# Linear ReLU attention: Q of the first octet loaded in fp32 on SP's queue

## The chip, the cores and the metric

The kernel runs on one core of a Trainium2 chip. The core has a matrix engine (TensorE, PE in the profile, with its weight loads as PEld), a vector engine (VectorE, DVE), a scalar engine (ScalarE, ACT), a general engine (GpSimd, POOL), a synchronising engine (SyncE, SP) and 16 DMA engines that move data between HBM and the on-chip memory SBUF. SP, ACT and POOL each issue DMA transfers on a queue of their own: q1 is SP's, q10 is ACT's and q0 is POOL's. PSUM is the memory that PE writes its results to.

The metric is the device time of one execution in microseconds; lower is better.

## The reference

```python
Q_feat = np.maximum(0, Q)
K_feat = np.maximum(0, K)
KV = np.einsum('bhkd,bhkv->bhdv', K_feat, V)
K_sum = np.sum(K_feat, axis=2)
numerator = np.einsum('bhqd,bhdv->bhqv', Q_feat, KV)
denominator = np.einsum('bhqd,bhd->bhq', Q_feat, K_sum)
return (numerator / (denominator[:, :, :, None] + 1e-10)).astype(np.float32)
```

Q, K and V are fp32 arrays of 8 batches x 12 heads x 512 rows x 64 values. That is 96 heads, 12.58 MB for each input and for the output.

## The kernel before

**Tiles.** Eight heads make an octet, and there are NO = 12 octets. An octet has two groups of four heads. K and V are loaded by group (g = 0 to 23): 128 partitions x 1024 values, which is 0.52 MB in HBM, in rows of 4 KB. Q is loaded by octet: 128 partitions x 2048 values, which is 1.05 MB in HBM, in rows of 8 KB. The output is stored by octet in the same form as Q.

**Loads.** POOL's DMAs (`load_kv`, lines 94 and 96, and `load_q`, line 100) cast fp32 to bf16 on the way, so they write half of the bytes that they read. K and V of the first two groups (F32 = 2) are the exception: SP loads K (line 106) and ACT loads V (line 107), both in fp32, into tiles `kv_first` that are borrowed from the pool `outp`, which later holds the output tiles `o_sb`. POOL's queue then runs in program order: Q of octet 0 (`load_q(0)`, line 108), the making of a bf16 identity matrix for transposes (`make_identity`, line 109), and for each octet from 1 to 11 two groups of K and V and then Q. The transfers of POOL's queue have eight semaphores in turn, so the ninth transfer is issued only when the first has landed, and so on. All of the instruction order is written out by hand (`manual_schedule`): each engine executes its instructions in the order of the program.

**Work on a group.** `prep(g)` (DVE, lines 136 and 138) takes relu of K with a mask per head into `kf` and copies one half of V into `vo`; `prep_v` (ACT, line 143, or DVE, line 145) copies the other half. `mm_kv(g)` (PE, line 150) multiplies 16 pairs of these into PSUM `ps_kv`, and `evac_kv` (ACT, line 160) copies the result into the bf16 tiles `kvd`. These are zeroed once, by DVE (`zero_kv`, line 129); in the order of DVE that stands after the work on groups 0 and 1 and after the fp32 identity `ident32` (line 259) and `mask_h` (line 261).

**Work on an octet.** `transp` (PE, line 171) transposes Q, two halves of 8 transposes each, into PSUM tiles `ps_qt` of the pool `pqt`. `relu_q` (ACT, line 179) takes relu of them into `qt`. `denom` (PE, line 210, then DVE, lines 213 to 222) computes the denominators and their reciprocals. `out_t` (PE, line 201, ACT, line 203) computes the transposed products in PSUM tiles of the pool `pou` (tag `ps_out`, two buffers) and copies them to SBUF. `back` (PE, line 228) transposes these in fp32 with `ident32` into tiles of the same tag, and `norm` (DVE, line 234) multiplies by the reciprocals into `o_sb`.

**Stores.** SP stores `o_sb` (line 249; the last octet in two halves, line 247). For octets 0 to 6 the store is preceded on SP's queue by a tiny transfer (line 242) that waits until K of the octet five further on (DELAY = 5) has landed. So the loads go ahead of the stores, and the stores of five octets are still to come when the loads are done.

**Order at the start.** PE runs `mm_kv(0)`, `mm_kv(1)`, then the transposes of Q of octet 0 and the steps above, octet by octet.

Of the kernel before, what the change touches and what calls it, by code (L numbers as in the profile page):

```python
# [10 lines left out]
def kernel(  # L11
# [7 lines left out]
    nc = tc.nc  # L19
    B, H, S, D = Q.shape  # L20
    assert D == 64
    P = 128
# [7 lines left out]
    U = RQ // 2  # L30
# [6 lines left out]
    fp32 = mybir.dt.float32  # L37
    bf16 = mybir.dt.bfloat16
# [3 lines left out]
    def pool(name, bufs, **kw):  # L42
        return ctx.enter_context(tc.tile_pool(name=name, bufs=bufs, **kw))
# [7 lines left out]
    outp = pool("outp", DELAY + 2)  # L51
    otp = pool("otp", 2)
    pkv = pool("pkv", 1, space=bass.MemoryType.PSUM)
    pqt = pool("pqt", 2, space=bass.MemoryType.PSUM)
    pde = pool("pde", 1, space=bass.MemoryType.PSUM)
    pou = pool("pou", 2, space=bass.MemoryType.PSUM)

    def view(X, f):
        return X.rearrange("b h s d -> (b h s d)").rearrange("(n p f) -> n p f", p=P, f=f)

    Qr, Kr, Vr, Or = view(Q, RQ * D), view(K, R * D), view(V, R * D), view(out, RQ * D)

    ident = consts.tile([P, P], bf16, name="ident")
    ident32 = consts.tile([P, P], fp32, name="ident32")
# [25 lines left out]
    q_sb, k_sb, v_sb = {}, {}, {}  # L90
# [7 lines left out]
    def load_q(o):  # L98
        q_sb[o] = qin.tile([P, U, 2 * D], bf16, name="q_sb")
        nc.gpsimd.dma_start(out=q_sb[o].rearrange("p u f -> p (u f)"), in_=Qr[o])  # L100


    for g in range(F32):
        kv = outp.tile([P, 2, R, D], fp32, name="kv_first", tag="o_sb")
        k_sb[g], v_sb[g] = kv[:, 0], kv[:, 1]
        nc.sync.dma_start(out=k_sb[g].rearrange("p r d -> p (r d)"), in_=Kr[g])
        nc.scalar.dma_start(out=v_sb[g].rearrange("p r d -> p (r d)"), in_=Vr[g])
    load_q(0)
    make_identity(nc, ident)
    for o in range(1, NO):  # L110
        load_kv(2 * o)
# [54 lines left out]


    def transp(o, i):
        ps = pqt.tile([P, U // 2, P], bf16, name="ps_qt")
        for u in range(U // 2):  # L170
            nc.tensor.transpose(ps[:, u, :], q_sb[o][:, i * (U // 2) + u, :], ident)  # L171
        return ps

    def relu_q(o, i, ps, eng=None):
# [6 lines left out]
    def qt(o):  # L181
        for i in range(2):
            relu_q(o, i, transp(o, i))
# [41 lines left out]
    def back(o, j):  # L225
        ps = pou.tile([P, 16, D], fp32, name="ps_bk", tag="ps_out")
        for v in range(8):
            nc.tensor.transpose(ps[:, 2 * v:2 * v + 2].rearrange("p c d -> p (c d)"),  # L228
                                ot[o][:, 8 * j + v].rearrange("p h c -> p (h c)"), ident32)
        return ps  # L230
# [20 lines left out]
    def out_tile():  # L251
        return outp.tile([P, RQ, D], fp32, name="o_sb", tag="o_sb")
# [50 lines left out]
    o = NO - 2  # L303
    g = 2 * NO - 2
# [9 lines left out]
    o_sb = out_tile()  # L314
    norm(o, 0, back(o, 0), o_sb)
    ps = back(o, 1)
    mm_kv(g + 1)
    evac_kv(o + 1, slice(1, 2), share=True)
    for i in range(2):
        relu_q(o + 1, i, transp(o + 1, i), nc.vector if i == 1 else None)  # L320
# [36 lines left out]
```

## Time and profile before

The runs took 126.66, 126.75 and 127.84 us; the median is 126.75 us. The profiled execution has a span of 124.8 us from its first instruction to its last; what a run takes beyond the span lies outside of it.

| what | in the profile before |
|---|---|
| median of the runs | 126.75 us |
| span of the profiled execution | 124.8 us |
| PE busy | 86.6 us (69%) |
| DVE busy | 81.1 us (65%) |
| ACT busy | 79.4 us (64%) |
| POOL busy | 31.2 us (25%) |
| DMA, bytes written | 32.68 MB, mean 262 GB/s |
| HBM read and written | 37.75 MB and 12.58 MB |
| POOL's queue q0 | 17.83 MB written |
| SP's queue q1 | 13.63 MB |
| ACT's queue q10 | 1.05 MB |

Busy time is the time in which an engine executes something; it is an average over stages that may have different limits. The DMA row of the page cuts the span into 40 slices and gives the mean busy share of the 16 DMA engines in tenths. GB/s counts written bytes; a casting load reads twice what it writes. A line of the timeline has the start in us, the duration, the engine, the line of the program, the operation, the tiles and, in brackets, how long the engine stood idle before and what ended that.

### The profile page before, as it was taken

The page shows a single profiled execution, that of the slowest core. Times are in us where ns is not written, and L with a number is a line of the kernel's source. Part 1 is how long each engine was busy: PE and PEld are TensorE (multiplying, and loading weights), DVE is VectorE, ACT ScalarE, POOL GpSimd, SP SyncE. Part 2 cuts the span into 40 slices and gives each one's busy share as a digit, 9 for nine tenths or more (in the row PEclk, how much of TensorE's full clock was granted, in tenths as well). Part 3 has the DMA queues.
Part 4 walks back from the last instruction along what each step waited for, and adds up shares of the span by engine and source line. Part 5 has one row for each costly group of instructions (what it writes and reads, how often), then busy time and mean ns, then how long its engine had stood idle before and what let it go on. Part 6 is the DMA issues. An engine that isn't in the chain of part 4 may idle for free.

```text
span 124.8 us, 2656 instructions
## 1 busy us (share of the span) xinstructions
PE 86.6 (69%) x1067; PEld 78.5 (63%) x1067; DVE 81.1 (65%) x176; ACT 79.4 (64%) x114; POOL 31.2 (25%) x62
## 2 busy tenths in 40 slices
PE   0032287998889899893598599399777577797600
PEld 0031285997878787792597499299576476695500
DVE  2257644759797997989147845934928918979430
ACT  0163369989898999988149558665939737737100
POOL 6902434314243331142133115034122000000000
PEclk9999999999999999999779859959999999999995
DMA  3999999999999999999999999999999999999993
GB/s 112 377 306 215 215 205 210 217 205 218 203 215 211 206 223 324 253 216 300 281 215 280 304 213 249 331 215 230 334 234 218 323 257 215 312 421 420 428 416 143
DMA packets 10748, 32.68 MB, mean 262 GB/s; under 512 B 1392, under 2 KB 1392, under 8 KB 9328
## 3 DMA queue, kind: packets, MB, share of 16 engines
q0 software_dynamic: 8064, 17.83, 74.7%
q1 hardware_dynamic: 2384, 13.63, 27.1%
q10 hardware_dynamic: 288, 1.05, 2.2%
q8 instruction: 8, 0.13, 0.4%
q14 instruction: 4, 0.03, 0.1%
HBM read 37.75 MB, written 12.58 MB: 403 GB/s over the span
## 4 chain that ended last, share of the span: by engine, by line
DMA 34%; DVE 30%; PE 23%; ACT 5%; issue 2%; DVEq 1%; SPq 0%; POOLq 0%; ACTq 0%
DMA v_sb<-in_V_dram 14%; DVE o_sb L234 13%; DMA q_sb<-in_Q_dram 13%; PE ps_kv L150 11%; DMA kv_first<-in_K_dram 7%; PE ps_bk L228 7%; DVE kf L136 5%; PE ps_qt L171 4%; DVE vo L138 3%; ACT kvd L160 2%; DVE vo L145 2%; PE ps_ot L201 2%; DVE den L218 2%; ACT qt L179 2%; DVE rec L222 1%
## 5 line engine op out<-in xcount | busy, mean ns | idle before, releaser
L150 PE MATMUL ps_kv<-vo,kf 128*128 128x132 bf16 x384 | 30.8, 244 | 17.7 <-ACT vo L143 8.2
L150 PEld LDWEIGHTS <-kf 128*128 128x128 bf16 x384 | 28.4, 110 | 19.0 <-DVE vo L138 10.9
L234 DVE TENSOR_TENSOR o_sb<-ps_bk,rec 128x1024 f32<-128x1024 f32 x24 | 28.3, 1219 | 17.1 <-PE ps_bk L228 17.1
L160 ACT CAST kvd<-ps_kv 64x260 bf16<-64x260 f32 (+1 forms) x54 | 18.7, 346 | 19.5 <-PE ps_kv L150 16.6
L203 ACT COPY ot_sb<-ps_ot 128x1024 f32<-128x1024 f32 x24 | 24.0, 1014 | 3.0 <-PE ps_ot L201 2.0
L179 ACT ACTIVATE qt<-ps_qt 128x1024 bf16<-128x1024 bf16 x23 | 22.4, 1026 | 5.6 <-PE ps_qt L171 5.5
L228 PE MATMUL ps_bk<-ident,ot_sb 128*128 128x128 f32 x192 | 23.0, 273 | 0.4 <-ACT ot_sb L203 0.4
L136 DVE TENSOR_SCALAR kf<-k_sb,mask 128x1024 bf16<-128x1024 bf16 x44 | 18.4, 460 | 6.4 <-DMA k_sb<-in_K_dram 6.3
L94 POOL DMA_DIRECT2D k_sb<-in_K_dram x22 | 11.9, 542 | 37.7 <-DMA q_sb<-in_Q_dram 24.1
L228 PEld LDWEIGHTS ps_bk<-ident,ot_sb 128*128 128x128 f32 x192 | 20.8, 141 | 0.7 <-ACT ot_sb L203 0.7
L171 PE MATMUL ps_qt<-ident,q_sb 128*128 128x128 bf16 x192 | 16.0, 250 | 6.0 <-DMA q_sb<-in_Q_dram 5.9
L171 PEld LDWEIGHTS <-q_sb 128*128 128x128 bf16 x192 | 14.3, 114 | 7.3 <-DMA q_sb<-in_Q_dram 7.1
L201 PE MATMUL ps_ot<-qt,kvd 128*128 128x256 bf16 x96 | 14.7, 283 | 5.0 <-DVE o_sb L234 4.3
L96 POOL DMA_DIRECT2D v_sb<-in_V_dram x22 | 12.3, 558 | 17.4 <-DMA k_sb<-in_K_dram 11.1
L201 PEld LDWEIGHTS <-kvd 128*128 128x128 bf16 x96 | 9.2, 101 | 7.8 <-issue 5.7
L138 DVE TENSOR_SCALAR vo<-v_sb,mask 128x1024 bf16<-128x1024 bf16 x22 | 10.6, 482 | 1.8 <-DMA v_sb<-in_V_dram 1.8
L143 ACT ACTIVATE vo<-v_sb,mask 128x1024 bf16<-128x1024 bf16 x10 | 11.5, 1152 | 0.2
L210 PEld LDWEIGHTS <-qt 128*128 128x128 bf16 x192 | 6.8, 97 | 4.4 <-ACT qt L179 3.4
L210 PE MATMUL ps_den<-kvd,qt 128*128 128x16 bf16 x192 | 7.5, 180 | 2.4 <-ACT qt L179 2.1
L100 POOL DMA_DIRECT2D q_sb<-in_Q_dram x12 | 6.6, 546 | 8.5 <-DMA v_sb<-in_V_dram 6.2
L213 DVE SCALAR_TENSOR_TENSOR own<-ps_den,mask_h 128x256 f32<-128x256 f32 x12 | 5.0, 417 | 3.3 <-PE ps_den L210 3.3
L136 DVE TENSOR_SCALAR kf<-kv_first,mask 128x1024 bf16<-128x1024 f32 x4 | 2.8, 749 | 5.1 <-DMA kv_first<-in_K_dram 5.1
(24 smaller groups left out, 28.3 us busy)
## 6 DMA issues: line engine op xcount, KB each, us to landing
out_dram<-o_sb SPq DMA_DIRECT2D x11, 1024.0 KB, 9.0
q_sb<-in_Q_dram POOLq DMA_DIRECT2D x12, 512.0 KB, 14.8
k_sb<-in_K_dram POOLq DMA_DIRECT2D x22, 256.0 KB, 14.1
v_sb<-in_V_dram POOLq DMA_DIRECT2D x22, 256.0 KB, 13.2
kv_first<-in_V_dram ACTq DMA_DIRECT2D x2, 512.0 KB, 7.2
kv_first<-in_K_dram SPq DMA_DIRECT2D x2, 512.0 KB, 6.9
out_dram<-o_sb SPq DMA_DIRECT2D x2, 512.0 KB, 4.3
scratch<-k_sb SPq DMA_DIRECT2D x7, 0.1 KB, 5.0
```

What stands on the lines that cost most here:

```text
L96: nc.gpsimd.dma_start(out=v_sb[g].rearrange("p r d -> p (r d)"), in_=Vr[g])
L136: nc.vector.tensor_scalar(kf[g][:, :, s, :], k_sb[g], scalar1=0.0, scalar2=mask[:, 0, s:s + 1], op0=Alu.max, op1=Alu.mult)
L138: nc.vector.tensor_scalar(vo[g % NB][:, :, 0, 2:D + 2], v_sb[g], scalar1=mask[:, 1, 0:1], scalar2=None, op0=Alu.mult)
L150: nc.tensor.matmul(ps_kv[:, g % 2, 0:2 * (D + 2)].rearrange("p (t d) -> p t d", t=2), kf[g][:, r, :, :].rearrange("p s d -> p (s d)"), vo[ ...
L160: copy(kvd[o % NK][64 * c:64 * c + 64, 4 * gs.start + s:4 * gs.stop:2, c * D1:c * D1 + D1].rearrange("p (g t) d -> p g t d", t=2), ps_kv[6 ...
L171: nc.tensor.transpose(ps[:, u, :], q_sb[o][:, i * (U // 2) + u, :], ident)
L179: nc.scalar.activation(to, ps, Act.Relu)
L201: nc.tensor.matmul(ps[:, i], kvd[o % NK][:, h, 1:2 * D + 1], q[:, :, h, :], start=True, stop=True, skip_group_check=True)
L203: nc.scalar.copy(ot[o][:, :, 4 * j:4 * j + 4], ps.rearrange("p h u c -> p u h c"))
L210: nc.tensor.matmul(ps[:, u], qt_sb[o % NZ][:, u, :], kvd[o % NK][:, :, 0:2 * D1:2 * D1 - 1], start=True, stop=True, skip_group_check=True)
L228: nc.tensor.transpose(ps[:, 2 * v:2 * v + 2].rearrange("p c d -> p (c d)"), ot[o][:, 8 * j + v].rearrange("p h c -> p (h c)"), ident32)
L234: nc.vector.tensor_tensor(o_sb[:, rs], ps, rec[o][:, rs].unsqueeze(2).to_broadcast([P, 16, D]), op=Alu.mult)
```

## The change

Q of octet 0 is no longer loaded by POOL with a cast. A tile `q_first` of the pool `outp` (same tag and size as `o_sb`) takes it in fp32, and SP loads it as its first transfer. K of group 0 moves from SP's queue to the head of ACT's, ahead of V of groups 0 and 1; K of group 1 stays on SP's queue, behind Q. On POOL's queue the making of the identity comes first, and then the loads from octet 1 on. The 16 transposes of octet 0 read fp32, use `ident32` in place of the bf16 identity, and write two fp32 tiles with the tag `ps_out` of the pool `pou`, which the products of `out_t` and `back` use as well. All other octets are as before. The lines after the change are numbered up to six higher than before.

```diff
--- before.py
+++ after.py
@@ -100,12 +100,15 @@
         nc.gpsimd.dma_start(out=q_sb[o].rearrange("p u f -> p (u f)"), in_=Qr[o])
 
 
+    q_first = outp.tile([P, U, 2 * D], fp32, name="q_first", tag="o_sb")
+    q_sb[0] = q_first
+    nc.sync.dma_start(out=q_first.rearrange("p u f -> p (u f)"), in_=Qr[0])
     for g in range(F32):
         kv = outp.tile([P, 2, R, D], fp32, name="kv_first", tag="o_sb")
         k_sb[g], v_sb[g] = kv[:, 0], kv[:, 1]
-        nc.sync.dma_start(out=k_sb[g].rearrange("p r d -> p (r d)"), in_=Kr[g])
+        eng = nc.scalar if g == 0 else nc.sync
+        eng.dma_start(out=k_sb[g].rearrange("p r d -> p (r d)"), in_=Kr[g])
         nc.scalar.dma_start(out=v_sb[g].rearrange("p r d -> p (r d)"), in_=Vr[g])
-    load_q(0)
     make_identity(nc, ident)
     for o in range(1, NO):
         load_kv(2 * o)
@@ -166,9 +169,12 @@
 
 
     def transp(o, i):
-        ps = pqt.tile([P, U // 2, P], bf16, name="ps_qt")
+        if o == 0:
+            ps = pou.tile([P, U // 2, P], fp32, name="ps_q0", tag="ps_out")
+        else:
+            ps = pqt.tile([P, U // 2, P], bf16, name="ps_qt")
         for u in range(U // 2):
-            nc.tensor.transpose(ps[:, u, :], q_sb[o][:, i * (U // 2) + u, :], ident)
+            nc.tensor.transpose(ps[:, u, :], q_sb[o][:, i * (U // 2) + u, :], ident32 if o == 0 else ident)
         return ps
 
     def relu_q(o, i, ps, eng=None):
```

## The prediction

> **What bounds the kernel now.** I read the page's DMA rows first, because the busiest engine, PE, fills only 69% of the span.
>
> ```profile
> DMA  3999999999999999999999999999999999999993
> HBM read 37.75 MB, written 12.58 MB: 403 GB/s over the span
> ```
>
> All 16 DMA engines work in every slice but the first and last. The traffic over HBM, 50.33 MB, is fixed by the inputs and the output. Next, the table by stretches (share of the DMA engines and GB/s stand last):
>
> ```profile
> 1.00:2.00 1.00, 0.00 (x0) 0.00 (x0) 0.44 (x9) 0.00 (x0) 0.76 (x2) 1.00 0.21 41
> 2.00:3.00 1.00, 0.00 (x0) 0.00 (x0) 0.17 (x2) 0.00 (x0) 0.93 (x4) 1.00 0.78 258
> 3.00:5.00 2.00, 0.00 (x0) 0.00 (x0) 0.00 (x0) 0.00 (x0) 2.00 (x4) 1.00 1.03 412
> ...
> 10.00:45.00 35.00, 27.15 (x349) 24.83 (x348) 26.11 (x59) 28.02 (x42) 12.60 (x23) 1.00 1.11 211
> 110.00:122.00 12.00, 6.90 (x86) 5.79 (x84) 7.10 (x11) 3.59 (x5) 0.00 (x0) 1.00 1.01 421
> ```
>
> GB/s counts bytes written. A casting load on POOL's queue writes half of what it reads, so 211 is 422 read. Fp32 loads give 412 and stores 421: whichever queue carries a byte, the rate is about 420. 50.33 MB at 420 GB/s are 119.8 us of the 124.8 us span; the rest is the ramp up to 3 us and the drain. The kernel is bound by DMA.
>
> Third, the DMA view of 5.3 to 9.5 us, where three queues compete (packets in all 324):
>
> ```profile
> q0 software_dynamic: 111, 0.45, 54.8%
> q10 hardware_dynamic: 114, 0.47, 27.5%
> q1 hardware_dynamic: 99, 0.37, 23.3%
> ```
>
> q0 is POOL's (here Q of octet 0, 8 KB read per row), q10 ACT's, q1 SP's (4 KB rows). The queues take turns by packet, so an 8 KB row gets twice the bytes of a 4 KB row. The same view of 1 to 5.3 us has no q0 at all: POOL issues Q at 1.24, and its data moves no sooner than 4.1 us later, while SP's and ACT's, issued at 0.74, start within about a microsecond.
>
> Fourth, the timeline of the start (start us, duration, engine, line; in brackets the idle time before and who ended it):
>
> ```profile
> 5.50 1.41 DVE L136 TENSOR_SCALAR kf<-kv_first,mask 128x1024 bf16<-128x1024 f32 x2 [3.12 <-DMA kv_first<-in_K_dram]
> 5.73 1.28 ACT L143 ACT_TABLE_LOAD   x1 [5.73 <-DMA kv_first<-in_V_dram]
> ...
> 10.25 1.42 DVE L136 TENSOR_SCALAR kf<-kv_first,mask 128x1024 bf16<-128x1024 f32 x2 [1.95 <-DMA kv_first<-in_K_dram]
> ...
> 13.61 1.09 ACT L160 CAST kvd<-ps_kv 64x130 bf16<-64x130 f32 x4 [1.71 <-DVE kvd L129]
> ...
> 14.76 1.92 PE L150 MATMUL ps_kv<-vo,kf 128*128 128x132 bf16 x16 [4.61 <-ACT kvd L160]
> ...
> 17.83 1.94 ACT L179 ACTIVATE qt<-ps_qt 128x1024 bf16<-128x1024 bf16 x2
> ```
>
> K of group 0 is there at 5.5, V at 5.7, K of group 1 at 10.25. Q of octet 0 is needed only at 16.5, long after it landed. Fifth, the Q transposes on PE in the timeline:
>
> ```profile
> 29.18 1.06 PE L171 MATMUL ps_qt<-ident,q_sb 128*128 128x128 bf16 x16
> ...
> 60.77 1.86 PE L171 MATMUL ps_qt<-ident,q_sb 128*128 128x128 bf16 x16 [2.89 <-DMA q_sb<-in_Q_dram]
> ...
> 80.77 1.42 PE L171 MATMUL ps_qt<-ident,q_sb 128*128 128x128 bf16 x16 [1.53 <-DMA q_sb<-in_Q_dram]
> ```
>
> Up to 50.8 they come every 7.1 to 7.3 us (29.18, 36.40, 43.49, 50.78): compute runs behind loads already landed. From 60.77 every 10.0 us, each time waiting for Q. The **slack** at 80.77 is 30.0 - 3 x 7.2 = 8.4 us: a start late by less than that is forgotten there. After 80.77 the chain of waits holds no DMA: compute at its own pace from that landing to the last stores.
>
> **The change part by part.**
>
> *Bytes.* Q of octet 0 moves from POOL's queue to SP's. It read 1.05 MB of HBM and still does; its writes double to 1.05 MB. At 412 GB/s (nearest: fp32 loads with 4 KB rows) 2.55 us, at 421 (stores, 8 KB rows) 2.49, as a casting load at 422 read 2.48. Cost 0.01 to 0.07; I take **+0.03**.
>
> *Ramp.* From 1 to 3 us 0.04 + 0.26 = 0.30 MB are moved; from 1.75 on, at 412 GB/s, it would be 0.51, so 0.5 us of transfer is lost. SP's first rows are now twice as long. If rows start as often as before, up to 0.5 us is gained; if the slow start is a rate of bytes, nothing; one slow 8 KB row per engine, at twice its measured 0.32 us, costs 0.3. The rows' start being the nearer reading, I take **-0.2** (bounds -0.5 to +0.3).
>
> *POOL.* It loses one DMA issue (L100, 0.66 us). The identity (0.22 + 0.29) comes first, and K of group 2 is issued at about 1.8 instead of 2.44. By the same 4.1 us its data starts at 5.9, when SP and ACT have 3.15 MB queued (to about 9.5 at 412): no gap, no gain. POOL keeps 8 transfers in flight by waiting on the eighth last; that goes on, one transfer further ahead. Cost 0. Were the cover gone, the late start would cost DMA idle time one for one.
>
> *What lands later.* SP: Q, K1. ACT: K0, V0, V1 (its three issues, 0.43 us each, delay nothing, since ACT first waits for V0). Until 5.0 us some 1.12 MB has moved; Q and K0 together are 1.57 MB, taking turns 2:1 in bytes, so both end near 6.1; landing is noticed 0.65 later (before: 1.05 MB at 4.85, used at 5.50). K0: 6.75. Then K1, V0 and POOL's K2 share equally, 137 GB/s each, 3.8 us: K1 and V0 at 10.55 (before 10.25 and 5.73). Then V1 at half the rate, 2.55 us: 13.1 (before 10.75).
>
> *The wait that follows.* ACT's table load and activation stand behind V0: 10.55 + 1.28 + 1.16 = 13.0, and the first K^T V product runs from 13.2 instead of 8.23, ending at 15.1. DVE, in order: vo0 to 11.3, the zeroing 0.7, kf1 1.4, vo1 0.75 (13.1 just met: 14.15), ident32 and mask_h 0.65, the kvd zeroing that the eviction waits for, 15.4. So L160 starts at 15.4 instead of 13.61: **1.8 us late**; mm_kv(1) to 18.5, its eviction to 19.6.
>
> *Fp32 transposes.* 8 of L228's take 0.89 us, 16 of L171's 1.06: fp32 costs 1.7 times as much, warm. Cold, 16 bf16 ones took 1.91, so 16 fp32 ones take 3.2 to 3.8; I take 3.6: 18.3 to 21.9. The relu of the second half then ends at 22.9; before, at 19.77. Start late by **3.1 us** (bounds 1.8, if the transposes hide behind the eviction, and 4.9, the delay of V0). Behind it on PE stand denom(0) and out_t(0), which need both halves anyway, so lending them the output PSUM tiles adds no wait. ident32 is ready at 14.3. Even 4.9 is less than 8.4: hidden by the DMA waits up to 80.77. First stores were issued at 43.5, some 15 us after their data, so they don't move.
>
> The page FP8 and Floating Point Precision of the Trainium skill (section TensorE Precision Notes) says that true fp32 takes 4 passes of the array, which speaks against fp32 transposes; the rows above show 1.7 times. By the page the 16 would take 7.6 us, the start would be 7.1 us late, still under 8.4, and the sum the same.
>
> The page DMA: Bandwidth & Descriptors (Specifications) puts the first byte of a POOL transfer at about 1 us; the trace shows 4.1 here. By the page K2 would take turns from 2.8 on, K0 would be about a microsecond later again, and the sum unchanged.
>
> **Sum.** Span 124.8 + 0.03 - 0.2 + 0 = 124.6. The median of the runs, 126.75, is 1.95 above the profiled span; with that, 126.55, say **126.5**; own range 126.2 to 127.1.
>
> **The rivals.**
>
> *Faster by over 1%.* The whole ramp (0.5), the first 3.15 MB at 421 instead of 412 (0.16), and a better aligned drain: the stores' engines now end raggedly after 122 us, worth perhaps 0.6. 126.75 - 1.3 = 125.4. For it: these losses are real. Against: nothing in the change touches the drain, and all three must come together.
>
> *Hidden anyway.* Bytes in the ramp limit, not rows: the same work in another order, 126.75. For it: engines are full from 3 us on.
>
> *Slower: a colder PE in the last stage.* The last store is issued with no queue left before it:
>
> ```profile
> 118.47 1.46 SPq L247 DMA_DIRECT2D out_dram<-o_sb  x2
> ```
>
> The engines thin out from 122, so compute after 80.77 is as critical as DMA. The table by stretches gives PE a granted clock of 0.80 from 60 to 84 us and 0.99 from 84 to 120. The PE pieces on the chain after 82 sum to 15.4 us; at 0.80 they'd cost 15.4 x 0.99/0.80 = 19.1, so +3.7: 130.4 from 126.75. It decides beyond 1% from a clock under 0.90 (15.4 x 0.99/0.90 = 16.9, the forecast's -0.2 made up and 1.3 added). For it: a shifted start shifts PE's pauses. Against: pauses shrink with a late start, and by 80.77 the old rhythm is back.
>
> *Slower: the start isn't forgotten.* Lag minus 8.4; with 10 us of lag 128.3. Nothing here makes V0 land that late.
>
> **How the numbers follow.** Forecast 0.58, hidden anyway 0.19, faster 0.06, colder last stage 0.13, unforgotten start 0.04. Within 1% is about what a measurement of this kernel can tell from no change: 0.77 for the first two, 0.06 faster, 0.17 slower. The range reaches from below 126.2 towards the faster case, 125.7, and up to 128.0, into the weaker half of the colder stage and the runs' own spread (126.66 to 127.84).
>
> **What would show it.** Right: K0 used near 6.8, V0 near 10.6, L160 first at 15 to 16, the first Q relu pair ending near 22 or 23, Q transposes again at 10.0 us intervals from about 61 to 81, and DMA full from 3 to 122 us. Wrong: a gap in the DMA rows at 6 to 10 us, V0 later than 12, transposes at 80 that no longer wait for Q, or a granted clock well under 0.99 after 84.

## The result, and the profile after

The changed kernel takes **127.48 us** (median; 127.38 to 127.72 over 12 runs), the kernel before 126.78 us (126.59 to 127.84 over 12 runs). The ratio is 1.0052, 95% interval 1.0036 to 1.0068: slower by 0.66 us, where 0.2 us faster was forecast. Comparisons here and below leave out executions that were disturbed.

The table by stretches of the profile after (PE's clock, DMA share and GB/s written at the end of each line), for the start and for a moment near the end:

```profile
1.00:2.00 1.00, 0.00 (x0) 0.00 (x0) 0.44 (x9) 0.00 (x0) 0.86 (x2) 1.00 0.18 33
2.00:3.00 1.00, 0.00 (x0) 0.00 (x0) 0.17 (x2) 0.00 (x0) 1.00 (x3) 1.00 0.48 147
3.00:5.00 2.00, 0.00 (x0) 0.00 (x0) 0.00 (x0) 0.00 (x0) 2.00 (x5) 1.00 0.98 399
...
120.00:121.00 1.00, 0.00 (x0) 0.00 (x0) 0.86 (x1) 0.00 (x0) 0.00 (x0) 1.00 0.74 307
```

The DMA engines start more slowly, not faster: a share of 0.48 in the third microsecond, where it was 0.78. From 1 to 5 us 0.033 + 0.147 + 2 x 0.399 = 0.98 MB are moved, against 1.12 MB before. At 420 GB/s the missing 0.145 MB are 0.35 us.

The start of the timeline after:

```profile
7.75 1.42 DVE L139 TENSOR_SCALAR kf<-kv_first,mask 128x1024 bf16<-128x1024 f32 x2 [5.37 <-DMA kv_first<-in_K_dram]
11.56 1.28 ACT L146 ACT_TABLE_LOAD   x1 [11.56 <-DMA kv_first<-in_V_dram]
...
16.40 1.09 ACT L163 CAST kvd<-ps_kv 64x130 bf16<-64x130 f32 x4 [1.33 <-DVE kvd L132]
...
19.26 3.10 PE L177 MATMUL ps_q<-ident,q_first 128*128 128x128 f32 x16
...
22.39 1.02 ACT L185 ACTIVATE qt<-ps_q 128x1024 bf16<-128x1024 f32 x1 [0.16 <-PE ps_q L177]
```

K of group 0 is used at 7.75 (forecast 6.8), V at 11.56 (10.6), the first eviction (the copy out of PSUM) runs at 16.40 (15.4), the fp32 transposes take 3.10 us (3.6), and Q of octet 0 is ready at 22.39 + 1.02 = 23.41 where it was 19.77: compute starts 3.6 us late (3.1 forecast). The later Q transposes show what becomes of that:

```profile
61.23 1.07 PE L177 MATMUL ps_qt<-ident,q_sb 128*128 128x128 bf16 x16 [1.07 <-DMA q_sb<-in_Q_dram]
71.22 1.89 PE L177 MATMUL ps_qt<-ident,q_sb 128*128 128x128 bf16 x16 [3.11 <-DMA q_sb<-in_Q_dram]
81.21 1.07 PE L177 MATMUL ps_qt<-ident,q_sb 128*128 128x128 bf16 x16 [0.76 <-DMA q_sb<-in_Q_dram]
```

From 61 us on they wait for Q again, every 10.0 us. The 3.6 us are gone, and what is left is 81.21 - 80.77 = 0.44 us, the delay of the loads. The best marker of the loads is the tiny transfer on SP's queue that waits for K of group 22, before the store of octet 6. SP's queue before, and then after:

```profile
102.85 0.50 SPq L242 DMA_DIRECT2D scratch<-k_sb  x1
103.45 11.23 SPq L249 DMA_DIRECT2D out_dram<-o_sb  x5
```

```profile
103.33 0.50 SPq L248 DMA_DIRECT2D scratch<-k_sb  x1
103.93 12.04 SPq L255 DMA_DIRECT2D out_dram<-o_sb  x5
119.76 1.46 SPq L253 DMA_DIRECT2D out_dram<-o_sb  x2
```

By this marker the loads are 0.48 us late. The last two stores are issued 1.29 us later than before (118.47), which makes the short gap at 120 us (share 0.74; before, 0.96). In this execution PE's granted clock (the figure ahead of the DMA share) was 0.50 from 108 to 110 us; I come back to that:

```profile
108.00:110.00 2.00, 2.00 (x16) 2.00 (x15) 1.78 (x5) 0.77 (x3) 0.00 (x0) 0.50 1.02 383
```

A second difference lies behind the last store. The waits of SP for the stores' landing, first in the profile before, then after (total us, times, longest):

```profile
SPq L352 <- DMA out_dram<-o_sb: 3.5, 3, 1.2
```

```profile
SPq L358 <- DMA out_dram<-o_sb: 3.3, 1, 3.3
```

The program ends with SP waiting for eight semaphores in a fixed order. SP's and ACT's transfers take them in turn, so the count of transfers decides on which of the eight the last store falls. Before, SP waits three times, as the last three stores land one after the other, and the last wait is the last semaphore. After, one long wait swallows them all: the last store is on the first semaphore. The trace's records of SP's semaphore instructions at the end (us):

```
before  ... 121.45  122.69  123.93 | drain 123.99
after   124.62 | 124.69 124.75 124.81 124.87 124.93 124.99 125.05 | drain 125.12
```

Seven waits for things long done, 0.061 us each, follow the last landing: 0.43 us. By the semaphore records the last store lands at 123.91 before and at 124.61 after, and the drain starts 0.08 and 0.51 us behind it. The change has five transfers on SP's and ACT's queues at the start where there were four, so 25 in the whole program where there were 24, three times eight.

### The profile page after: what moved, and what is told of

The parts are those of the page before. It is cut to its first block, busy times and chain, and to the rows that moved or that the text cites. A ratio compares the mean times of both kernels' runs of the same rounds, so it can differ in the third digit from the quotient of the medians.

```text
span 125.9 us, 2657 instructions
## 1 busy us (share of the span) xinstructions
PE 85.5 (68%) x1067; PEld 77.7 (62%) x1067; DVE 81.0 (64%) x176; ACT 79.2 (63%) x114; POOL 30.6 (24%) x61
## 4 chain that ended last, share of the span: by engine, by line
DMA 77%; PE 7%; DVE 6%; issue 2%; POOL 1%; ACT 1%; DVEq 1%; POOLq 0%
DMA k_sb<-in_K_dram 30%; DMA q_sb<-in_Q_dram 26%; DMA v_sb<-in_V_dram 21%; DVE o_sb L240 4%; PE ps_bk L234 4%; PE ps_kv L153 2%; DVEq L358 1%; PE ps_qt L177 1%; ACT ot_sb L209 1%; DVE kf L139 1%; DVE qt L183 1%; POOL k_sb L94 1%; PE ps_ot L207 0%; DVE kvd L163 0%; ACT kvd L163 0%
## 5 line engine op out<-in xcount | busy, mean ns | idle before, releaser
L153 PE MATMUL ps_kv<-vo,kf 128*128 128x132 bf16 x384 | 30.1, 241 | 21.0 <-ACT vo L146 14.1
L153 PEld LDWEIGHTS <-kf 128*128 128x128 bf16 x384 | 27.5, 107 | 22.3 <-DVE vo L141 13.2
L234 PE MATMUL ps_bk<-ident,ot_sb 128*128 128x128 f32 x192 | 23.8, 279 | 0.4 <-ACT ot_sb L209 0.4
L185 ACT ACTIVATE qt<-ps_qt 128x1024 bf16<-128x1024 bf16 x21 | 20.5, 1026 | 4.4 <-PE ps_qt L177 4.4
L234 PEld LDWEIGHTS ps_bk<-ident,ot_sb 128*128 128x128 f32 x192 | 21.6, 145 | 0.7 <-ACT ot_sb L209 0.7
L207 PE MATMUL ps_ot<-qt,kvd 128*128 128x256 bf16 x96 | 14.0, 271 | 5.5 <-DVE o_sb L240 4.8
L177 PE MATMUL ps_qt<-ident,q_sb 128*128 128x128 bf16 x176 | 12.5, 228 | 5.6 <-DMA q_sb<-in_Q_dram 5.6
L177 PEld LDWEIGHTS <-q_sb 128*128 128x128 bf16 x176 | 11.0, 102 | 6.8 <-DMA q_sb<-in_Q_dram 6.6
L100 POOL DMA_DIRECT2D q_sb<-in_Q_dram x11 | 6.0, 545 | 9.9 <-DMA v_sb<-in_V_dram 8.4
```

What stands on the lines that cost most here:

```text
L153: nc.tensor.matmul(ps_kv[:, g % 2, 0:2 * (D + 2)].rearrange("p (t d) -> p t d", t=2), kf[g][:, r, :, :].rearrange("p s d -> p (s d)"), vo[ ...
L185: nc.scalar.activation(to, ps, Act.Relu)
L207: nc.tensor.matmul(ps[:, i], kvd[o % NK][:, h, 1:2 * D + 1], q[:, :, h, :], start=True, stop=True, skip_group_check=True)
```

## The experiments

Ratios are to the kernel before, with 95% intervals.

**E1: rows of 4 KB.**

```diff
-    nc.sync.dma_start(out=q_first.rearrange("p u f -> p (u f)"), in_=Qr[0])
+    qf = q_first.rearrange("p u f -> p (u f)")
+    for h in range(2):
+        c = slice(h * RQ * D // 2, (h + 1) * RQ * D // 2)
+        nc.sync.dma_start(out=qf[:, c], in_=Qr[0][:, c])
```

> The changed kernel with its first Q transfer on SP cut in two, so that its rows are 4 KB instead of 8 KB; bytes, queue and order are the same. Theory R (the ramp: 8 KB rows at the very start are handed to the DMA engines more slowly, and a kernel bound by DMA never gets that back): the DMA share from 2 to 3 us goes from 0.48 back to 0.70 or more, the Q transposes of octet 8 start near 80.8 instead of 81.2, and the time falls by 0.3 to 0.5 us, ratio to the kernel before 1.001 to 1.003. Rival T (PE's lower granted clock near 107 us delays the last stores): row size is no part of it, the ratio stays at 1.005 unless the clock happens to hold.

Measured: 1.0121 (1.0108 to 1.0134), worse instead of better. The table by stretches:

```profile
2.00:3.00 1.00, 0.00 (x0) 0.00 (x0) 0.17 (x2) 0.00 (x0) 1.00 (x3) 1.00 0.66 106
3.00:5.00 2.00, 0.00 (x0) 0.00 (x0) 0.00 (x0) 0.00 (x0) 2.00 (x5) 1.00 0.95 305
```

The engines are busy, but move 305 GB/s where they moved 399 and 412; the marker before octet 6's store goes to 104.18. So shorter rows in this form don't bring the start back: theory R falls in that form. The two halves differ from the single transfer not only in the length of the rows but also in count and in leaving out every other 4 KB of Q; which of these costs isn't settled, so E1 doesn't test the length alone.

**E2: extra matmuls to hold PE's clock.**

```diff
         if o >= SAME:
+            idle(6, o)
             kvs(o + 1)
...
     out_t(o)
+    idle(6, o)
     mm_kv(g)
```

> The changed kernel with six extra idle matmuls on PE at two places late in the program (in the last turns of the loop before the K^T V products, and before those of group 22), in gaps in which PE waits for VectorE. Theory T: the granted clock stays near 1.0 from 106 to 112 us, the last stores are issued near 118.5 instead of 119.8, and the time comes back to a ratio of 1.000 to 1.002. Theory R: the loads are as late as in the changed kernel (transposes of octet 8 near 81.2), so only the gap in the stores near 120 us closes, about 0.2 us: ratio 1.003 to 1.004.

Measured: 1.0117 (1.0087 to 1.0147), with runs from 127.54 to 130.89. The timeline of one of the longer ones (129.84 us) shows a new wait:

```profile
98.18 1.44 PE L194 MATMUL ps_den<-q_sb,ident 128*128 128x256 bf16 x6 [0.80 <-DVE own L219]
...
108.63 1.44 PE L194 MATMUL ps_den<-q_sb,ident 128*128 128x256 bf16 x6 [1.20 <-DVE own L219]
```

The idle matmuls write the tile of the denominators and so had to wait for VectorE's reading of it, and the products behind them with them. The last stores were issued from 121.86 on. Nor did the clock hold: it averaged 0.90 from 84 to 120 us, where the changed kernel had 0.95. So the new waits and the colder PE can't be told apart, and the test of theory T failed; all it shows is that a last stage as late as that does cost time.

**E3: Q last on SP's queue.**

```diff
-    nc.sync.dma_start(out=q_first..., in_=Qr[0])
     for g in range(F32):
...
-        eng = nc.scalar if g == 0 else nc.sync
-        eng.dma_start(out=k_sb[g]..., in_=Kr[g])
+        nc.sync.dma_start(out=k_sb[g]..., in_=Kr[g])
...
+    nc.sync.dma_start(out=q_first..., in_=Qr[0])
     make_identity(nc, ident)
```

> The changed kernel with Q of octet 0 as the last of SP's first transfers instead of the first, and K of group 0 back on SP ahead of it; 8 KB rows, fp32 transposes and the order on POOL's queue are kept. Theory R: the first transfers are those of the kernel before, so the DMA share from 2 to 3 us is 0.75 or more and the ratio 0.999 to 1.001. A rival, that fp32 on SP's queue or the fp32 transposes cost the time themselves: ratio 1.004 to 1.006 still.

Measured: 1.0045 (1.0033 to 1.0057). The start is nearly as it was before (share 0.78 from 2 to 3 us, marker at 103.05), and yet 0.57 us are lost. That sent me to the end of the program.

**E4: the fp32 path alone, by POOL.**

```diff
-    nc.sync.dma_start(out=q_first..., in_=Qr[0])
+    nc.gpsimd.dma_start(out=q_first..., in_=Qr[0])
...
-        eng = nc.scalar if g == 0 else nc.sync
-        eng.dma_start(out=k_sb[g]..., in_=Kr[g])
+        nc.sync.dma_start(out=k_sb[g]..., in_=Kr[g])
```

> Only the fp32 half of the change: Q of octet 0 is loaded without a cast by POOL, in its old place, and transposed in fp32 into the output products' PSUM tiles; SP and ACT load K and V as in the kernel before. If the fp32 path is free (the step of the prediction), ratio 0.999 to 1.001, with the transposes taking some 3 us instead of 1.9. If the fp32 path is what costs, ratio 1.004 to 1.006.

Measured: 0.9997 (0.9988 to 1.0006). The fp32 transposes cost no time in the end, though they take nearly twice the 1.91 us of before:

```profile
16.48 3.58 PE L176 MATMUL ps_q<-ident,q_first 128*128 128x128 f32 x16
```

This kernel has four transfers on SP and ACT at the start, as before, and its waits at the end are those of before (3.6 us in 3 waits).

**F1: one tiny transfer more, in the kernel before.**

```diff
+    for i in range(1):
+        tiny = consts.tile([1, D], fp32, name=f"tiny{i}")
+        nc.sync.dma_start(out=tiny, in_=Kr[i][0:1, 0:D])
     make_identity(nc, ident)
```

> The kernel before with one more transfer of 256 bytes on SP's queue behind its first loads; nothing else is changed. Theory S (the count of transfers on SP's and ACT's queues moves the last store to another of eight semaphores, and SP, which at the end waits for the eight in their order, then still has seven waits of 0.06 us to go through after the last store has landed): 7 x 0.061 = 0.43 us more, ratio 1.0034; in the trace the waits of SP end some 0.45 us after the last store landed, the loads being as before. Rival: the loss comes from the loads at the start alone, and a tiny transfer costs nothing: ratio 1.000.

Measured: 1.0040 (1.0026 to 1.0054). 256 bytes cost 0.51 us. Its marker and its waits:

```profile
102.93 0.50 SPq L245 DMA_DIRECT2D scratch<-k_sb  x1
```

```profile
SPq L355 <- DMA out_dram<-o_sb: 3.3, 1, 3.3
```

The loads are as before, and the end is that of the changed kernel: one long wait, then seven more, with the drain 0.51 us behind the last landing. The profiled execution is the slowest of the seven (127.51 us, median 127.25): its last stores were issued 1.07 us later than in the profile before, and the last one landed 0.48 us later (124.39). This one trace is thus 0.91 us longer, 0.48 of later landing and 0.43 of waits; the 0.51 us of the median is close to the waits alone.

**F4: four tiny transfers, in the kernel before.** The edit of F1 with `range(4)`.

> The kernel before with four transfers of 256 bytes on SP's queue behind its first loads. Theory S: the last store falls on the fourth of the eight semaphores, four waits remain: 4 x 0.061 = 0.24 us, ratio 1.0019, between the kernel before and the form with one tiny transfer, although there are more of them. Rival, that each tiny transfer costs: more than the form with one. Rival, that they are free: 1.000.

Measured: 1.0019 (1.0007 to 1.0030), the 0.24 us of theory S. Four transfers cost no more than one, so it isn't their cost; four waits were left after the last landing (123.96), and the drain came 0.32 us behind it.

**F2: seven tiny transfers, in the changed kernel.** The edit of F1 with `range(7)`.

> The changed kernel with seven transfers of 256 bytes on SP's queue behind its first loads, so that the last store falls on the same semaphore as in the kernel before. Theory S: 0.43 us comes back, ratio 1.001 to 1.003; what is left is the slower start of the loads (some 0.3 us). Rival: the start explains the whole 0.7 us, and seven tiny transfers can only add: ratio 1.005 or more.

Measured: 1.0036 (1.0023 to 1.0049), less of a gain than expected, its interval overlapping that of the change. H2 repeats the test with the changed kernel beside it.

**F3: E3 with seven tiny transfers.**

> Q of octet 0 in fp32 as the last of SP's first transfers, and seven transfers of 256 bytes behind it. Theory S with the start repaired: nothing is left of the loss, ratio 0.999 to 1.001 (this form without the tiny transfers had 1.0045). Rival, that Q on SP's queue costs the time by itself: 1.004 to 1.005 still.

Measured: 1.0009 (0.9999 to 1.0020). With the start nearly and the end fully as before, 0.11 us is left, which the interval doesn't tell from nothing: Q in fp32 on SP's queue costs little or nothing in itself.

**G1: only K of group 0 moved to ACT's queue, in the kernel before.**

```diff
-        nc.sync.dma_start(out=k_sb[g]..., in_=Kr[g])
+        eng = nc.scalar if g == 0 else nc.sync
+        eng.dma_start(out=k_sb[g]..., in_=Kr[g])
```

> The kernel before with K of group 0 moved from SP's queue to the head of ACT's, as in the change; Q of octet 0 stays with POOL and the count of transfers on SP and ACT is that of the kernel before. Theory Q (it is Q of octet 0 at the head of a queue that makes the start slow): the DMA share from 2 to 3 us stays at 0.75 or more and the ratio is 0.999 to 1.001, although V of group 0 comes 2 us or more later and the first K^T V product with it. Rival L (the later K and V, and so the later compute, cost the time): ratio 1.002 to 1.004 with a normal start of the loads.

Measured: 0.9999 (0.9986 to 1.0011). V of group 0 is used at 9.05 instead of 5.73, the first product starts at 11.56 instead of 8.23, and nothing comes of it. The share from 2 to 3 us was 0.55, not the 0.75 expected, but the bytes are nearly there:

```profile
1.00:2.00 1.00, 0.00 (x0) 0.00 (x0) 0.43 (x9) 0.00 (x0) 0.77 (x2) 1.00 0.66 57
2.00:3.00 1.00, 0.00 (x0) 0.00 (x0) 0.17 (x2) 0.00 (x0) 0.92 (x4) 1.00 0.55 188
3.00:5.00 2.00, 0.00 (x0) 0.00 (x0) 0.00 (x0) 0.00 (x0) 2.00 (x4) 1.00 1.01 410
```

0.057 + 0.188 + 2 x 0.410 = 1.07 MB, marker at 102.86. Bytes are the better measure of a start than the busy share.

**G2: Q second on SP's queue, seven tiny transfers.**

```diff
         nc.scalar.dma_start(out=v_sb[g]..., in_=Vr[g])
+        if g == 0:
+            nc.sync.dma_start(out=q_first..., in_=Qr[0])
```

(with K of both groups on SP, Q no longer first, and the seven tiny transfers of F2)

> Q of octet 0 in fp32 as SP's second transfer, behind K of group 0 and ahead of K of group 1; V of both groups on ACT; seven transfers of 256 bytes behind them, so that the last store falls on the last of the eight semaphores. Theory Q: the start is as in the kernel before (share 0.75 or more from 2 to 3 us), ratio 1.000 to 1.002. If Q ahead of K of group 1 costs in itself, as with Q first: ratio 1.003 to 1.004.

Measured: 1.0011 (1.0001 to 1.0020). Q behind K of group 0 costs 0.14 us, Q ahead of it (F2) 0.46.

**H1 and H2: the changed kernel again, and with the tiny transfers late.**

```diff
+        if o == 1:
+            for i in range(7):
+                tiny = consts.tile([1, D], fp32, name=f"tiny{i}")
+                nc.sync.dma_start(out=tiny, in_=Kr[i][0:1, 0:D])
         Ov = Or[o].rearrange("p (r d) -> p r d", d=D)
```

> The changed kernel itself, as the partner of the next one on the same chip: ratio 1.004 to 1.006 to the kernel before by every theory; the DMA share from 2 to 3 us is again 0.5 or less if the slow start belongs to Q at the head of SP's queue and not to one profile.

> The changed kernel with seven transfers of 256 bytes ahead of the store of octet 1 (near 54 us), where DMA is full anyway; the start is untouched, and the last store falls on the last of the eight semaphores as in the kernel before. Theory S: 0.43 us less than the changed kernel beside it, so a ratio lower by 0.003: 1.001 to 1.003, the rest being the slow start. If the place of the last store among the semaphores is worth less in the changed kernel than in the kernel before: 1.004.

Measured: H1 1.0059 (1.0042 to 1.0076), H2 1.0030 (1.0018 to 1.0043), in one series on one chip. The slowest run of H2 (127.31 us) is faster than the fastest of H1 (127.38). The difference, 0.0029, is 0.37 us: theory S, for the changed kernel too. In the traces the last store lands at 124.35 in H1 and 124.25 in H2, and the drain comes 0.51 and 0.08 us behind it. The rest, 0.0030, is 0.38 us (0.23 to 0.55): the start. H1's table by stretches:

```profile
1.00:2.00 1.00, 0.00 (x0) 0.00 (x0) 0.43 (x9) 0.00 (x0) 0.86 (x2) 1.00 1.02 131
2.00:3.00 1.00, 0.00 (x0) 0.00 (x0) 0.17 (x2) 0.00 (x0) 1.00 (x3) 1.00 0.34 49
...
108.00:110.00 2.00, 2.00 (x27) 2.00 (x25) 1.95 (x6) 1.45 (x5) 0.00 (x0) 1.00 1.00 371
```

PE's clock is 1.00 from 84.4 us to the last matmul in this execution, its last stores are issued at 118.78 instead of 119.76, and it takes 127.48 us, the median of the first series. The first profile's execution, with the colder PE, took 127.71 us, and its last store landed 0.26 us later than H1's. So the colder PE is worth some 0.2 us between these two executions, and the loss is there without it.

All together, the bytes moved from 1 to 5 us, the marker of the loads (ready for the store of octet 6), the waits left after the last landing, and the time:

| kernel | first on SP | MB, 1 to 5 us | marker, us | waits left | ratio |
|---|---|---|---|---|---|
| before | K | 1.12 | 102.85 | 0 | 1 |
| G1 | K | 1.07 | 102.86 | 0 | 0.9999 |
| E4 | K | 1.02 | 103.04 | 0 | 0.9997 |
| F4 | K | 1.11 | 102.90 | 4 | 1.0019 |
| F1 | K | 1.12 | 102.93 | 7 | 1.0040 |
| F3 | K | 1.05 | 103.17 | 0 | 1.0009 |
| E3 | K | 1.05 | 103.05 | 7 | 1.0045 |
| H2 | Q | 0.95 | 103.22 | 0 | 1.0030 |
| F2 | Q | 0.96 | 103.40 | 0 | 1.0036 |
| after | Q | 0.98 | 103.33 | 7 | 1.0052 |
| H1 | Q | 0.98 | 103.34 | 7 | 1.0059 |
| E1 | Q, 4 KB | 0.76 | 104.18 | 6 | 1.0121 |

Waits left times 0.061 us plus the delay of the marker give the loss to within 0.25 us in every row. For E1: 0.37 + 1.33 = 1.70 us, measured 1.53. That is coarse beside losses of a few tenths, since each marker and each count of bytes comes from a single execution: F3 (103.17) and H2 (103.22) hardly differ in them. What separates them is the time. With no waits left, the kernels that begin with K have 0.9997 to 1.0011 (G1, E4, F3, G2), those that begin with Q 1.0030 and 1.0036 (H2, F2).

The DMA records agree that the loss is made at the start. Counted by what is read, H1 is 0.14 MB behind the kernel before at 5 us and still 0.145 MB behind at 20 us: the deficit neither grows nor is made up. At 20 us the five profiles with Q's 8 KB rows first stand at 7.15 to 7.19 MB, the seven of the table that begin with K at 7.24 to 7.35.

None of these kernels beats the kernel before.

## Why the prediction was wrong

**The bound was right.** DMA sets the time, and no byte was added or taken away. The steps built on that held. The late start of compute was forecast at 3.1 us and measured at 3.6, and the DMA waits hid it up to 80.77 as worked out; G1 and E4 show that the later V and the fp32 transposes cost nothing on their own. K and V landed about a microsecond later than forecast; 0.35 us of that is the slower ramp. POOL's earlier loads brought nothing, as said (F3).

**The ramp term failed.** It was taken as -0.2 us, with bounds of -0.5 and +0.3. It is +0.38 (H2, 0.23 to 0.55): the other sign, around the far bound or beyond it. The step that failed is the choice that rows would start as often as before, so that longer rows gain. The five profiles with Q's 8 KB rows first have 0.95 to 0.98 MB after 5 us, the kernels that begin with K 1.02 to 1.12. One slow row per engine had been priced at twice the steady 0.32 us. In the trace of H1 the sixteen first rows of Q take 0.55 to 1.36 us each, and the seventeenth begins only at 3.0 us; in the first profile four rows begin at 1.8, the next four at 2.1 to 2.2 and the others from 2.6 on. In the five profiles the seventeenth row of SP's queue begins at 2.8 to 3.1 us, in those with K first at 2.0 to 2.5. I named the mechanism as a bound, but sized it by rows of steady traffic, not by those of the start.

**One term was missing.** The sum took what follows the last store as fixed. It changed by 0.43 us in the traces (0.37 us by the time of H2 beside H1, 0.51 by that of F1) through a count that the prediction never made: five transfers on SP's and ACT's queues for four. The count could be made from the kernels before the run: the last store is the 24th transfer in the kernel before and takes the eighth semaphore; after the change it is the 25th and takes the first. The two terms together, 0.38 + 0.37 = 0.75 us, are the loss of H1.

**The rivals.** "Hidden anyway" came nearest in time and mechanism, 0.7 us off. The colder PE did occur in the profiled execution, at 107 to 110 us (0.95 from 84 to 120 us), and its last stores came 1.3 us later. But its rival's premise, that the last store is issued with no queue left before it, misread the profile before: the store of octet 10 landed there only at 121.44, some 3 us after the first half of octet 11's was issued at 118.47, and this queue covered most of the delay. 127.48 lies in the outer range, though above the sum's own (126.2 to 127.1), and within 1%, where most of the chance lay; the sign was wrong. That it came so near is no merit of the sum, which had one of the two terms with the wrong sign and lacked the other.

**Still open:** why Q at the head of SP's queue starts more slowly than K does. E1 speaks against row length but changed the count and the pitch with it, and slow first rows aren't Q's alone: in G1 the first sixteen rows of K, 4 KB each, took 0.59 to 0.86 us. Whether it is the length of the rows by itself, where Q lies in HBM, or the pairing of Q with K on the other queue, was not tried.

## What to carry to other kernels

When DMA is full from start to end and moves the same bytes at the same rate, what is left to change the time is what happens before it is full and after its last byte, so look there first: count the bytes of the first microseconds, and follow the program past the last store. In a program that ends like this one, adding or removing a single transfer can move the last store to another semaphore and change the end by up to seven waits of 0.06 us; before blaming an edit for a few tenths, add a transfer of 256 bytes to the kernel without it. Delays in compute ahead of a stretch that waits for loads cost nothing as long as that stretch has slack for them (here 3.6 us late, 8.4 us of slack by the prediction's count).

## What the runs showed of the hardware

One more 256-byte transfer on SP's queue cost 0.51 us (F1), four of them 0.24 (F4): the price is in SP's waits at the end, 0.061 us each, not in the transfer.

At the very start, DMA engines can count as fully busy and move little: in H1 the share is 1.02 from 1 to 2 us, at 131 GB/s, and 0.34 in the next, at 49.

With Q read as two transfers of every other 4 KB, all queues together moved 305 GB/s from 3 to 5 us, beside 399 with Q in one transfer of 8 KB rows.

PE's granted clock was 1.0 or 0.5 in the clock records of the changed kernel's two profiles, and its low stretches fell at different places in them: from 107.0 to 110.4 us in the first, nowhere from 84.4 us to the last matmul in H1.
